# Later scale matmuls and later weight splits in the first MLP product, and an earlier g_mem_post product in the memory rows

## The chip, the cores and the metric

The kernel runs on one core of one Trainium2 chip. The metric is the device time of one execution in microseconds (us), measured over several runs of the same program; a further execution is profiled. The engines are TensorE (PE in the profile), VectorE (DVE), ScalarE (ACT), GpSimd (POOL) and SyncE (SP), whose queue here issues the loads and stores.

## The reference

One layer of a streaming encoder, on x of 1024 rows by 1024 columns. In outline:

```
x = x + rmsnorm(concat(rmsnorm(fox), rmsnorm(chunked)) @ w_out, g_mix_post)   # two attention groups
h = rmsnorm(x, g_mem_pre)
y = memory_cross_attention(h, rmsnorm(mem, g_mem_kv), w_mq, w_mk, w_mv, w_mo) # 4 heads, 256 memory rows
x = x + rmsnorm(y, g_mem_post)
h = rmsnorm(x, g_ff_pre)
y = square(relu(h @ w_ff1)) @ w_ff2                                           # 1024 -> 4096 -> 1024
x = x + rmsnorm(y, g_ff_post)
```

`rmsnorm(x, g)` is x / sqrt(mean(x^2) + 1e-6) * g. All inputs and the result are float32. The change touches the end of the memory attention (its norm, the residual, the next norm) and the first product of the MLP, here FF1.

## The kernel before, in words

A float32 product is made of three float16 ones: each operand is split into a high part (ACT's activation, `split_hi`, L2520) and a low part, value minus high part (DVE, `split_lo`, L2523), and `mm3` (L230 to L232) sums high x high, low x high and high x low in one PSUM bank. Before it is split a weight is multiplied by a scale that comes from its squares. FF1 and FF2 are moreover done by a two by two scheme with seven products in place of eight, so sums of operands and results (s1 to s4, u2, u3, g11, g22) stand on DVE and POOL.

Up to the memory attention a planner sets the order of the work. The part here, from the last rows of the memory attention on, is written under `tc.manual_schedule()`: each engine does its instructions in the order in which the program text issues them, and an instruction that waits holds up all that stands behind it on its engine. The same is true of SP's queue.

**The rows.** The second half of the rows comes in four blocks b of 128. For each, `ym` is a product of 24 matmuls; `row_out` (L2696 to L2700) squares it on ACT (L1248), multiplies its right half by g_mem_post on DVE (L2699) and takes the inverse root of the mean square on POOL (h3y, L1253 to L1256). `row_sum` (L2702 to L2707) adds it to the residual `xth` on DVE (L2703), stores the sum and squares it on ACT, and POOL takes the next inverse root (h3x). `row_norm` (L2710) multiplies by it and by g_ff_pre. `residual_in` loads `xth`. Then the rows are transposed (`Turn`, PE's trx), and summed and split for the seven products.

**FF1.** The 4096 columns are worked as 16 pairs j of two blocks of 128, a pair in seven products of 12 matmuls. `first_row` makes the first two, px and py; for pairs 0 to 6 (`AHEAD` = 7) they are made early, between the rows, and put by; from pair 7 on at the head of the pair. Then come the products T2 (into px, and from pair 7 on added to what px holds), T1 (into pz), T3 (px), T4 (pv) and B22 (pz). ACT copies px out three times: p (L2583), u after T2 (L2986) and u after T3 (L3004; before pair 7 DVE's L3002 stands for it). DVE then makes g22 from pz and that u (L3006). `Weights` holds the weights of a pair: `squares` (ACT, jn, L2771), `scales` (PE's nw of two small matmuls, L2777; DVE's rowsc, L2778; POOL's roots and factors, L2779 to L2782), and `split(n)` for n = "a" (whi_a, wlo_a), "s23" (v..hi, v..lo), "s1a" and "s4" (u..hi, u..lo). While pair j is worked, pair j+1's weights are scaled and split, and pair j+2's are squared; two rows of FF2's weights are squared in each pair too (w2n, L1311). At pair 14 the norms of all features and of FF2's weights are taken (L1384 to L1401).

Of the kernel before, what the change touches and what calls it, by code (L numbers as in the profile page):

```python
# [165 lines left out]
def layer(tc, out, t):  # L166
    nc = tc.nc
    ctx = ExitStack()
    with ctx:
        build(ctx, tc, nc, out, t)  # L170


def build(ctx, tc, nc, out, t):
# [13 lines left out]
    def mm_tile(shape, name, tag="mm"):  # L187
        return psp.tile(shape, F32, tag=tag, bufs=2, name=name)
# [39 lines left out]
    def mm3(ps, lh, ll, rh, rl, start, stop, more=False):  # L228

        nc.tensor.matmul(ps, lh, rh, start=start, stop=False, skip_group_check=more)  # L230
        nc.tensor.matmul(ps, lh, rl, start=False, stop=False, skip_group_check=more)  # L231
        nc.tensor.matmul(ps, ll, rh, start=False, stop=stop, skip_group_check=more)  # L232
# [1013 lines left out]
    def square_sum(x, ss, n=1024, scale=1.0 / 32.0):  # L1246
        junk = p2.tile([P, D], BF16, tag="junk", bufs=1, name="junk")
        nc.scalar.activation(junk[:, :n], x, AF.Square, scale=scale, accum_out=ss)  # L1248

    def inverse_rms(a, name, b=None):  # L1250
        r = small.tile([P, 1], F32, tag="rstd", bufs=8, name=name)
        if b is None:
            nc.gpsimd.tensor_scalar(r, a, EPS, None, op0=ALU.add)  # L1253
        else:
            nc.gpsimd.tensor_scalar(r, a, b, EPS, op0=ALU.add, op1=ALU.add)
        nc.gpsimd.tensor_tensor(r, r, mhalf[:, 0:1], op=ALU.pow)  # L1256
        return r
# [979 lines left out]
    with tc.manual_schedule():  # L2237
# [87 lines left out]
        ps = mm_tile([P, 4], "ssx", "pv")  # L2325
# [149 lines left out]
    AHEAD = 7  # L2475
# [6 lines left out]
    def t2(name):  # L2482
        if region[0]:
            return pr.tile([P, HT], F32, tag="t2", bufs=9, name=name)
        return pf.tile([P, HT], F32, tag="t2", bufs=18, name=name)
# [3 lines left out]
    def bank(name, tag=None):  # L2489
        if tag is None:  # L2490
            tag = ("mm", "s", "tr", "pv")[banks[0] % 4]
            banks[0] += 1
        return mm_tile([P, HT], name, tag)
# [12 lines left out]
    def raw_w(src, name):  # L2506
        raw = wp.tile([P, D], F32, tag="wraw", bufs=3, name=name)
        nc.sync.dma_start(raw, src)
        return raw
# [20 lines left out]
    def product(ps, w, off, blk, more=False):  # L2530
        for kc in range(4):
            c = slice(off + kc * P, off + (kc + 1) * P)
            xh, xl = blk.at(kc)
            mm3(ps, w.hi[:, c], w.lo[:, c], xh, xl, kc == 0 and not more, kc == 3, more)

    def ff1_raw(fb):
        return raw_w(t["w_ff1"][fb].rearrange("p a b -> p (a b)"), f"wf{fb}")
# [154 lines left out]
    def residual_in(b):  # L2692
        xts[b] = p2.tile([P, D], F32, tag="xt", bufs=2, name=f"xth3{4 + b}")
        nc.sync.dma_start(xts[b], x1d[4 + b])

    def row_out(b, ps):  # L2696

        square_sum(ps, ss[b][:, 1:2], HT, um32)
        nc.vector.tensor_tensor(y[b][:, HT:], ps, gmpost[:, HT:], op=ALU.mult)  # L2699
        rx[b] = inverse_rms(ss[b][:, 0:1], f"h3y{4 + b}", ss[b][:, 1:2])  # L2700

    def row_sum(b):  # L2702
        nc.vector.scalar_tensor_tensor(xts[b], y[b], rx[b], xts[b], op0=ALU.mult, op1=ALU.add)  # L2703
        nc.sync.dma_start(x2d[4 + b], xts[b])
        s2 = small.tile([P, 1], F32, tag="ss", bufs=8, name=f"s2h3{4 + b}")
        square_sum(xts[b], s2)
        rx[b] = inverse_rms(s2, f"h3x{4 + b}")  # L2707

    def row_norm(b):
        nc.vector.scalar_tensor_tensor(y[b], xts[b], rx[b], gffpre, op0=ALU.mult, op1=ALU.mult)  # L2710

    manual = ExitStack()
    manual.enter_context(tc.manual_schedule())
    residual_in(0)
    raws = {}
    for b in range(4):
        c = slice(b * P, (b + 1) * P)
        ps = mm_tile([P, HT], f"ym11{b}", "tr" if b < 2 else "pv")
        for kp in range(4):
            for j in range(2):  # L2720
                mm3(ps, o[kp][0][:, j, c], o[kp][1][:, j, c], wo[kp][0][:, j, :], wo[kp][1][:, j, :],
                    kp == 0 and j == 0, kp == 3 and j == 1)
        if b:
            row_sum(b - 1)
            row_norm(b - 1)
        if b < 3:
            raws[EARLY + b] = ff1_raw(EARLY + b)
            residual_in(b + 1)
            row_out(b, ps)
    units = [Turn(a, i) for a in range(2) for i in range(2)]  # L2730
    add = {}
    units[0].turn()
    row_out(3, ps)
    units[0].sums()
    add[0] = ahead(0)
    row_sum(3)
# [82 lines left out]
    cur, nxt = Weights(0), Weights(1)  # L2819
# [128 lines left out]
    with manual:  # L2948
        sums, stores, norms, puts = (lambda: []), [], [], []
        for j in range(NP):  # L2950
            more = j + 1 < NP
            after = Weights(j + 2) if j + 2 < NP else None
            w = cur.w
            late = more and 0 < j < AHEAD
# [20 lines left out]
                fetch(3)  # L2975
                prepare(0)
            product(x, w["s23"], 0, XT["T2"], more=j >= AHEAD)
            if more and j + 1 >= AHEAD:
                nxt.scales()
            put_off = j < PUT_OFF  # L2980
            both = u4(f"ug{j}", (P, 2, HT), F32) if put_off else None
            u2 = both[:, 0, :] if put_off else t2(f"u2_{j}")
# [6 lines left out]
            put(j, 0, g11)  # L2989
            z = bank(f"pz{j}")  # L2990
            product(z, w["s1a"], 0, XT["T1"])
            if late:
                nxt.sums(nc.vector)
            if more:
                if j + 1 >= AHEAD:
                    nxt.split("a")
                if j and not late:
                    nxt.split("s23")
            product(x, w["s23"], HT, XT["T3"], more=True)
            u3 = p1 if put_off else t2(f"u3_{j}")  # L3000
            if j < AHEAD:
# [2 lines left out]
                nc.scalar.activation(u3, x, AF.Copy)  # L3004
            g22 = both[:, 1, :] if put_off else t2(f"g22_{j}")
            nc.vector.tensor_add(g22, z, u3)  # L3006
            stores = [form() for form in forms[:1]]
            if late:
                nxt.sum4(nc.vector)
# [60 lines left out]
            cur, nxt = nxt, after  # L3070
# [266 lines left out]
```

## Time and profile before

| | us |
|---|---|
| median of 3 runs (lowest to highest) | 1436.27 (1435.35 to 1437.5) |
| the profiled execution | 1439.24 |
| its span | 1437.4 |
| PE busy in it | 1398.9 (97%) |
| DVE, ACT, POOL busy | 1163.8 (81%), 1010.9 (70%), 527.4 (37%) |
| mean granted clock of PE | 0.992 |

A share of busy time is a mean over stages. What an edit is worth is read where it stands: which engine waits there, for what, and what comes after. In a row of the trace the first figure is the start in us from the span's start, the second the duration, then come engine, line, operation, written tile, read tiles and shape; in brackets the idle time of that engine before it and what ended that time. The row blocks lie at 780 to 860 us, the early first products up to some 880, the pairs 0 to 6 up to 979, the pairs 7 to 15 up to some 1150; FF2 follows to the end.

### The profile page before, as it was taken

To read this page: it belongs to the slowest core of one execution; us is meant where nothing else is said; L and a number is where in the kernel's file an instruction comes from. 1 tells how busy PE (TensorE), PEld (TensorE's weight loads), DVE (VectorE), ACT (ScalarE), POOL (GpSimd) and SP (SyncE) were. 2 spreads that over 40 slices of the span, in tenths; PEclk is the share of its full clock that TensorE was granted. 3 is DMA by queue.
4 is the path that set the end of the run, shared out by engine and by line. 5 is a ranking of instruction groups with operands and counts; after the bars stand their busy time and mean duration, and the time that the engine had idled before them with its cause. 6 is when DMAs were issued, how large, how long until landed. Compare 5 with 4: busy or idle time off the path is not lost. (4 is left out here: it accounts for less than half of the span.)

```text
span 1437.4 us, 22722 instructions
## 1 busy us (share of the span) xinstructions
PE 1398.9 (97%) x7723; PEld 866.2 (60%) x7723; DVE 1163.8 (81%) x1886; ACT 1010.9 (70%) x1750; POOL 527.4 (37%) x679
## 2 busy tenths in 40 slices
PE   8989999999999999999999999999999999999997
PEld 8746666666668887855556544444444445666653
DVE  7887877777778755889888877777988987899998
ACT  6767888978778775686466555786887657665654
POOL 2467777787655433451113421003344100000003
PEclk9999999999999999999999999999999999999999
DMA  7142454345424566461325446976888998686885
GB/s 281 49 128 75 131 165 165 112 122 164 137 74 139 174 233 235 174 235 49 103 81 169 143 170 241 339 240 203 271 289 281 323 382 306 238 306 224 312 300 205
DMA packets 116214, 286.31 MB, mean 199 GB/s; under 512 B 13161, under 2 KB 31601, under 8 KB 116097
## 3 DMA queue, kind: packets, MB, share of 16 engines
q1 hardware_dynamic: 115952, 284.59, 58.7%
q8 instruction: 61, 1.00, 0.3%
q14 instruction: 57, 0.46, 0.1%
q10 hardware_dynamic: 144, 0.26, 0.1%
HBM read 210.82 MB, written 65.59 MB: 192 GB/s over the span
## 5 line engine op out<-in xcount | busy, mean ns | idle before, releaser
L3104 POOL TENSOR_SCALAR rf<-sf 128x1 f32<-128x1 f32 x7 | 6.4, 912 | 280.7 <-ACT jf L3083 280.4
L870 ACT ACTIVATE phl<-ptr 128x512 f16<-128x512 f32 (+3 forms) x152 | 80.9, 537 | 38.4 <-PE ptr L860 35.7
L1910 POOL TENSOR_SCALAR mp<-mp,mst 128x256 f32<-128x256 f32 x32 | 22.6, 716 | 121.1 <-DVE mst L1909 110.1
L866 DVE SCALAR_TENSOR_TENSOR phl<-ptr,phl 128x384 f16<-128x384 f32 (+1 forms) x76 | 46.8, 617 | 14.9 <-ACT phl L870 14.2
L868 DVE TENSOR_TENSOR phl<-ptr,phl 128x384 fp32r<-128x384 f32 (+1 forms) x76 | 46.5, 617 | 9.5 <-ACT phl L870 8.8
L230 PE MATMUL yw<-whiwo,yT_hi 128*128 128x512 f32 x128 | 51.3, 401 | 2.7 <-DVE yw L1625 2.7
L2943 ACT ACTIVATE vhif<-ra,fsc 128x1024 f16<-128x1024 f32 x34 | 38.9, 1143 | 19.4 <-PE fx L232 9.2
L2943 ACT ACTIVATE whif<-ra,fsc 128x1024 f16<-128x1024 f32 x34 | 38.9, 1144 | 19.3 <-PE fx L232 12.0
L2945 DVE SCALAR_TENSOR_TENSOR vhif<-ra,fsc,vhif 128x1024 f16<-128x1024 f32 x34 | 43.6, 1282 | 10.0 <-ACT vhif L2943 9.7
L907 PE MATMUL pv<-phl,vs 128*128 128x512 f32 (+1 forms) x152 | 50.9, 421 | 0.0
L231 PE MATMUL yw<-wlowo,yT_hi 128*128 128x512 f32 x128 | 50.6, 395 | 0.0
L232 PE MATMUL yw<-whiwo,yT_lo 128*128 128x512 f32 x128 | 50.4, 394 | 0.0
L230 PE MATMUL q<-hF_hi,wq 128*128 128x512 f16 x128 | 49.0, 383 | 0.7 <-DVE qs L1011 0.7
L230 PE MATMUL fx<-vlof,vhif 128*128 128x512 f16 x128 | 48.5, 379 | 0.8 <-DVE yc L3155 0.8
L230 PE MATMUL k<-hF_hi,wk 128*128 128x512 f16 x128 | 49.3, 385 | 0.0
L231 PE MATMUL q<-hF_lo,wq 128*128 128x512 f16 x128 | 48.5, 379 | 0.6 <-DVE hF_lo L2231 0.6
L231 PE MATMUL k<-hF_lo,wk 128*128 128x512 f16 x128 | 49.0, 383 | 0.0
L2945 DVE SCALAR_TENSOR_TENSOR whif<-ra,fsc,whif 128x1024 f16<-128x1024 f32 x34 | 43.6, 1281 | 6.4 <-ACT whif L2943 6.3
L232 PE MATMUL k<-hF_hi,wk 128*128 128x512 f16 x128 | 48.8, 381 | 0.0
L232 PE MATMUL q<-hF_hi,wq 128*128 128x512 f16 x128 | 48.5, 379 | 0.2 <-POOL wq L571 0.2
L230 PE MATMUL fx<-wlof,whif 128*128 128x512 f16 x128 | 48.5, 379 | 0.0
L231 PE MATMUL fx<-wlof,whif 128*128 128x512 f16 x128 | 48.5, 379 | 0.0
(906 smaller groups left out, 5372.3 us busy)
## 6 DMA issues: line engine op xcount, KB each, us to landing
wg<-in_w_ff SPq DMA_DIRECT2D x48, 512.0 KB, 5.7
ra<-gd SPq DMA_DIRECT2D x40, 512.0 KB, 5.3
wf<-in_w_ff SPq DMA_DIRECT2D x38, 512.0 KB, 4.4
w2n<-in_w_ff SPq DMA_DIRECT2D x32, 512.0 KB, 5.5
wi<-in_w_ff2q SPq DMA_DIRECT2D x28, 512.0 KB, 6.0
gd<-s SPq DMA_DIRECT2D x32, 256.0 KB, 5.0
wn<-in_w_ff SPq DMA_DIRECT2D x14, 512.0 KB, 4.5
gd<-g SPq DMA_DIRECT2D x19, 256.0 KB, 4.5
```

The lines of the kernel that those rows point to most:

```text
L230: nc.tensor.matmul(ps, lh, rh, start=start, stop=False, skip_group_check=more)
L231: nc.tensor.matmul(ps, lh, rl, start=False, stop=False, skip_group_check=more)
L232: nc.tensor.matmul(ps, ll, rh, start=False, stop=stop, skip_group_check=more)
L866: flow.put("V", at, 0.68, lambda: nc.vector.scalar_tensor_tensor(pl[:, live, :], tr[:, live, :], 2.0 ** 14, ph[:, live, :], op0=ALU.mult, ...
L868: if ph.dtype == F16 else nc.vector.tensor_sub(pl[:, live, :], tr[:, live, :], f(ph[:, live, :])), done, 1)
L870: flow.put("S", flow.end, 0.6, lambda ph=ph, tr=tr, live=live: nc.scalar.activation(ph[:, live, :], tr[:, live, :], AF.Copy, scale=2.0 ** ...
L907: nc.tensor.matmul(pv[:, :, qs_, :], v, hl[:, :, hs, :], start=c == 0 and turn == 0, stop=last)
L1910: mul = lambda st=st, pr=pr: nc.gpsimd.tensor_scalar(pr, pr, st[:, 2:3], 1.0, op0=ALU.mult, op1=ALU.mult)
L2943: nc.scalar.activation(ah, ra, AF.Copy, scale=su)
L2945: nc.vector.scalar_tensor_tensor(al, ra, su, ah, op0=ALU.mult, op1=ALU.subtract)
L3104: nc.gpsimd.tensor_scalar(r, ssf[b][:, 0:1], ssf[b][:, 1:2], EPS, op0=ALU.add, op1=ALU.add)
```

## The change

Two things are moved; nothing is added and nothing is taken away.

In the row blocks, the product with g_mem_post of block b+1 (`row_out`) stands ahead of the norm of block b (`row_norm`), the sum of a block follows at once, and the residual of block 1 is loaded together with that of block 0. In FF1, for pairs 6 to 14, `nxt.scales()` stands behind the T1 product and no longer behind the T2 product, and the splits "a" and "s23" of the next pair stand behind the T3 product's reading (u and g22) and no longer before it.

```diff
--- before.py
+++ after.py
@@ -2712,6 +2712,7 @@
     manual = ExitStack()
     manual.enter_context(tc.manual_schedule())
     residual_in(0)
+    residual_in(1)
     raws = {}
     for b in range(4):
         c = slice(b * P, (b + 1) * P)
@@ -2720,17 +2721,18 @@
             for j in range(2):
                 mm3(ps, o[kp][0][:, j, c], o[kp][1][:, j, c], wo[kp][0][:, j, :], wo[kp][1][:, j, :],
                     kp == 0 and j == 0, kp == 3 and j == 1)
-        if b:
-            row_sum(b - 1)
-            row_norm(b - 1)
         if b < 3:
+            row_out(b, ps)
+            if b:
+                row_norm(b - 1)
+                residual_in(b + 1)
             raws[EARLY + b] = ff1_raw(EARLY + b)
-            residual_in(b + 1)
-            row_out(b, ps)
+            row_sum(b)
     units = [Turn(a, i) for a in range(2) for i in range(2)]
     add = {}
+    row_out(3, ps)
+    row_norm(2)
     units[0].turn()
-    row_out(3, ps)
     units[0].sums()
     add[0] = ahead(0)
     row_sum(3)
@@ -2975,8 +2977,6 @@
                 fetch(3)
                 prepare(0)
             product(x, w["s23"], 0, XT["T2"], more=j >= AHEAD)
-            if more and j + 1 >= AHEAD:
-                nxt.scales()
             put_off = j < PUT_OFF
             both = u4(f"ug{j}", (P, 2, HT), F32) if put_off else None
             u2 = both[:, 0, :] if put_off else t2(f"u2_{j}")
@@ -2989,13 +2989,10 @@
             put(j, 0, g11)
             z = bank(f"pz{j}")
             product(z, w["s1a"], 0, XT["T1"])
+            if more and j + 1 >= AHEAD:
+                nxt.scales()
             if late:
                 nxt.sums(nc.vector)
-            if more:
-                if j + 1 >= AHEAD:
-                    nxt.split("a")
-                if j and not late:
-                    nxt.split("s23")
             product(x, w["s23"], HT, XT["T3"], more=True)
             u3 = p1 if put_off else t2(f"u3_{j}")
             if j < AHEAD:
@@ -3004,6 +3001,11 @@
                 nc.scalar.activation(u3, x, AF.Copy)
             g22 = both[:, 1, :] if put_off else t2(f"g22_{j}")
             nc.vector.tensor_add(g22, z, u3)
+            if more:
+                if j + 1 >= AHEAD:
+                    nxt.split("a")
+                if j and not late:
+                    nxt.split("s23")
             stores = [form() for form in forms[:1]]
             if late:
                 nxt.sum4(nc.vector)
```

DVE at the last three row blocks, before (xth is the residual and sum, ym the product, L2699 the g_mem_post product, L2703 the sum, L2710 the norm):

```order
L2703 SCALAR_TENSOR_TENSOR xth_9891<-ym_9370,h3y_9925,xth_9891 128x1024
L2710 SCALAR_TENSOR_TENSOR ym_9370<-xth_9891,h3x_9958,g_ff_pre 128x1024
L2699 TENSOR_TENSOR ym_9371<-ym_9928,g_mem_post 128x512
L2703 SCALAR_TENSOR_TENSOR xth_9920<-ym_9371,h3y_9969,xth_9920 128x1024
L2710 SCALAR_TENSOR_TENSOR ym_9371<-xth_9920,h3x_10002,g_ff_pre 128x1024
L2699 TENSOR_TENSOR ym_9372<-ym_9972,g_mem_post 128x512
L2703 SCALAR_TENSOR_TENSOR xth_9964<-ym_9372,h3y_10013,xth_9964 128x1024
L2710 SCALAR_TENSOR_TENSOR ym_9372<-xth_9964,h3x_10046,g_ff_pre 128x1024
L2699 TENSOR_TENSOR ym_9373<-ym_10016,g_mem_post 128x512
```

and now:

```order
L2703 SCALAR_TENSOR_TENSOR xth_9891<-ym_9370,h3y_9923,xth_9891 128x1024
L2699 TENSOR_TENSOR ym_9371<-ym_9936,g_mem_post 128x512
L2710 SCALAR_TENSOR_TENSOR ym_9370<-xth_9891,h3x_9933,g_ff_pre 128x1024
L2703 SCALAR_TENSOR_TENSOR xth_9893<-ym_9371,h3y_9964,xth_9893 128x1024
L2699 TENSOR_TENSOR ym_9372<-ym_9980,g_mem_post 128x512
L2710 SCALAR_TENSOR_TENSOR ym_9371<-xth_9893,h3x_9977,g_ff_pre 128x1024
L2703 SCALAR_TENSOR_TENSOR xth_9968<-ym_9372,h3y_10008,xth_9968 128x1024
L2699 TENSOR_TENSOR ym_9373<-ym_10024,g_mem_post 128x512
L2710 SCALAR_TENSOR_TENSOR ym_9372<-xth_9968,h3x_10021,g_ff_pre 128x1024
```

The product L2699 of a block moved from behind the norm L2710 of the block before to ahead of it.

PE in pair 6, at the end of the T2 product (px) and the beginning of the T1 product (pz), before:

```order
L231 MATMUL px_11158<-T_lo,v0hi_s_11098 128x512
L232 LDWEIGHTS v0lo_s_11099
L232 MATMUL px_11158<-T_hi,v0lo_s_11099 128x512
L2777 MATMUL nw_11171<-wsq,o_83 128x1 x2
L230 LDWEIGHTS whi_s1a_11121
L230 MATMUL pz_11189<-T_hi,whi_s1a_11121 128x512
```

and now, at the end of the T1 product and the beginning of the T3 product (px):

```order
L231 MATMUL pz_11181<-T_lo,whi_s1a_11121 128x512
L232 LDWEIGHTS wlo_s1a_11122
L232 MATMUL pz_11181<-T_hi,wlo_s1a_11122 128x512
L2779 MATMUL nw_11194<-wsq,o_83 128x1 x2
L230 LDWEIGHTS v0hi_s_11098
L230 MATMUL px_11158<-T_hi,v0hi_s_11098 128x512
```

The small matmuls nw moved behind 12 matmuls.

ACT in pair 8, from the end of g11 on, before (L3004 is the copy u after T3, whi_a and v1hi are split high parts of pair 9's weights, w2n squares):

```order
L2541 ACTIVATE g_8_11499<-g_8_11499 128x512
L2520 ACTIVATE whi_a_11552<-wf_11284,rowsc 128x1024
L2520 ACTIVATE v1hi_s_11556<-sc_11453,rowsc 128x1024
L3004 ACTIVATE u_8_11572<-px_11471 128x512
L1311 ACTIVATE w2n_11286,wsq<-w2n_11286 128x1024
L1311 ACTIVATE w2n_11288,wsq<-w2n_11288 128x1024
L2520 ACTIVATE whi_s1a_11601<-wf_11395,rowsc 128x1024
L2540 ACTIVATE g_8_11574<-g_8_11574,rowsc 128x512
L2541 ACTIVATE g_8_11574<-g_8_11574 128x512
```

and the same place now, where the copy is L3001:

```order
L2541 ACTIVATE g_8_11499<-g_8_11499 128x512
L3001 ACTIVATE u_8_11564<-px_11471 128x512
L2520 ACTIVATE whi_a_11568<-wf_11284,rowsc 128x1024
L2520 ACTIVATE v1hi_s_11572<-sc_11453,rowsc 128x1024
L1311 ACTIVATE w2n_11286,wsq<-w2n_11286 128x1024
L1311 ACTIVATE w2n_11288,wsq<-w2n_11288 128x1024
L2520 ACTIVATE whi_s1a_11601<-wf_11395,rowsc 128x1024
L2540 ACTIVATE g_8_11566<-g_8_11566,rowsc 128x512
L2541 ACTIVATE g_8_11566<-g_8_11566 128x512
```

The copy u moved ahead of the two split parts, which stand behind it now. The order behind these rows, up to the squares jn and the copy p of pair 9's px, is the same in both.

DVE from g11 of pair 7 (L2585) to the low parts of pair 8, before (rowsc is made from nw, g by L3006 is g22):

```order
L2585 TENSOR_TENSOR g_7_11318<-py_11303,p_7_11316 128x512
L2778 TENSOR_SCALAR rowsc<-nw_11332 128x1
L3050 TENSOR_TENSOR s_6_11344<-u_6_11179,g_6_11224 128x512
L3056 TENSOR_TENSOR u_6_11179<-p1r_11104,u_6_11179 128x512
L3058 TENSOR_TENSOR s_6_11347<-s_6_11344,p1r_11104 128x512
L3060 TENSOR_TENSOR s_6_11348<-u_6_11222,s_6_11347 128x512
L2523 SCALAR_TENSOR_TENSOR wlo_a_11372<-wf_11152,rowsc,whi_a_11371 128x1024
L2523 SCALAR_TENSOR_TENSOR v0lo_s_11376<-sc_11278,rowsc,v0hi_s_11375 128x1024
L3006 TENSOR_TENSOR g_7_11393<-pz_11358,u_7_11391 128x512
```

and now, with all lines behind the moved text two or three numbers off (rowsc L2780, the sums L3052 to L3062, g22 L3003):

```order
L2585 TENSOR_TENSOR g_7_11318<-py_11303,p_7_11316 128x512
L3052 TENSOR_TENSOR s_6_11336<-u_6_11171,g_6_11220 128x512
L3058 TENSOR_TENSOR u_6_11171<-p1r_11104,u_6_11171 128x512
L3060 TENSOR_TENSOR s_6_11339<-s_6_11336,p1r_11104 128x512
L3062 TENSOR_TENSOR s_6_11340<-u_6_11218,s_6_11339 128x512
L2780 TENSOR_SCALAR rowsc<-nw_11363 128x1
L3003 TENSOR_TENSOR g_7_11385<-pz_11350,u_7_11383 128x512
L2523 SCALAR_TENSOR_TENSOR wlo_a_11388<-wf_11152,rowsc,whi_a_11387 128x1024
L2523 SCALAR_TENSOR_TENSOR v0lo_s_11392<-sc_11278,rowsc,v0hi_s_11391 128x1024
```

rowsc moved behind the four sums, and g22 ahead of the two low parts.

## The prediction

> **What bounds the kernel now.** I read the page first, then TensorE's waits stage by stage, then the instructions around each of those waits. The page says that TensorE (PE) is the engine that sets the time:
>
> ```profile
> span 1437.4 us, 22722 instructions
> PE 1398.9 (97%) x7723; PEld 866.2 (60%) x7723; DVE 1163.8 (81%) x1886; ACT 1010.9 (70%) x1750; POOL 527.4 (37%) x679
> ```
>
> PE is idle for 38.5 us of 1437.4, so only what removes or adds PE idle time (or halves its clock) counts. PE's waits in the two stretches that the change touches, first 780 to 880 us (rows of the memory attention and the first rows of FF1), then 960 to 1130 us (pairs 6 to 14 of FF1), then all that follows:
>
> ```profile
> PE px L230 <- ACT whi_a L2520: 2.3, 1, 2.3
> PE px L232 <- DVE wlo_a L2523: 0.7, 1, 0.7
> ...
> PE nw L2777 <- ACT jn L2771: 1.8, 2, 1.0
> PE pz L230 <- DVE g L3006: 1.3, 2, 1.0
> ...
> PE py L230 <- DVE fsc L1384: 0.5, 1, 0.5
> ```
>
> The columns are total, times, longest. Waits that the edits can reach come to some 6 us; that is all there is to win beside the clock. Nothing in a stretch of 170 us with 1.3 us of `pz` waits leaves room for a large gain, but anything that comes late there is paid in full.
>
> **Term 1, the rows.** The product with g_mem_post (L2699) now stands ahead of the norm (L2710). One row of before on DVE, ACT and POOL:
>
> ```profile
> 826.39 1.28 DVE L2703 SCALAR_TENSOR_TENSOR xth<-ym,h3y,xth 128x1024 f32<-128x1024 f32 x1
> 829.92 1.29 DVE L2710 SCALAR_TENSOR_TENSOR ym<-xth,h3x,g_ff_pre 128x1024 f32<-128x1024 f32 x1 [2.25 <-POOL h3x L1256]
> 831.12 0.69 DVE L2699 TENSOR_TENSOR ym<-ym,g_mem_post 128x512 f32<-128x512 f32 x1
> 832.05 1.28 DVE L2703 SCALAR_TENSOR_TENSOR xth<-ym,h3y,xth 128x1024 f32<-128x1024 f32 x1 [0.25 <-POOL h3y L1256]
> ...
> 829.53 0.19 ACT L1248 ACTIVATION_READ_ACCUMULATOR junk<-ym,mfx 128x1 f32 x1
> ...
> 829.00 0.23 POOL L1253 TENSOR_SCALAR h3x<-s2h 128x1 f32<-128x1 f32 x1 [4.31 <-ACT junk L1248]
> 829.98 1.39 POOL L1255 TENSOR_SCALAR h3y<-ssm 128x1 f32<-128x1 f32 x1
> 831.46 0.56 POOL L1256 TENSOR_TENSOR h3y<-h3y,mhalf 128x1 f32<-128x1 f32 x1
> ```
>
> A row takes 832.05 - 826.39 = 5.66 us. POOL's small h3y operation takes 1.39 beside the norm where its like for h3x takes 0.23 alone, and the next sum waits for it. In the new order the product waits for ACT's square of the same bank (829.53 + 0.19 = 829.72), starts at about 829.75 and gives way to the norm 0.60 later, at 830.35 instead of 829.92. By then POOL's h3y operation has run unhindered (from 829.9, with some 0.1 between operations) and its root, 0.56, is just begun; the norm is issued over in 1.20 (831.12 - 829.92), so the next sum comes at 831.55 instead of 832.05. That is 0.5 us a row, for two rows, and 0.2 at the last one, about 1.2 us at the sums of the first turn. If the norm wins against the root, the root is done after it and nothing is gained.
>
> The Trainium skill, "SBUF — State Buffer", Who interferes with whom, says that a VectorE operation with two SBUF inputs and a GpSimd one exclude each other and that whoever issues first runs whole. The 1.39 against 0.23 agrees with it; it makes this term 1.2 or 0 by a margin of about 0.1 us.
>
> What it is worth to PE is less. PE is next late for the split weights of row 3 (the 2.3 and 0.7 above), and after that DVE has hardly a gap, as busy times by stretch show (PE, PEld, DVE, ACT, POOL, granted clock, DMA share, GB/s):
>
> ```profile
> 858.80:864.80 6.00, 6.00 (x15) 2.14 (x16) 5.91 (x9) 1.56 (x4) 0.00 (x0) 0.50 0.72 204
> ```
>
> I take -0.8 (between -1.2 and 0). The earlier residual load (xth1) only moves ahead of two weight loads on SP's queue; the first of PE's needs of those is not late in the waits above, so it is 0. The 0.50 clock costs some 3 us here; a wait shortened from 2.3 to 1.5 might avoid it (to -4), a chance I keep for the range.
>
> **Term 2, pair 6.** Before the z product PE stands for the squares of pair 7:
>
> ```profile
> 964.64 0.38 PE L232 MATMUL px<-T_hi,v0lo_s 128*128 128x512 f16 x1
> 965.98 0.38 PE L2777 MATMUL nw<-wsq,o 128*128 128x1 f32 x2 [0.95 <-ACT jn L2771]
> 967.16 0.58 PE L2777 MATMUL nw<-wsq,o 128*128 128x1 f32 x2 [0.80 <-ACT jn L2771]
> 971.65 0.38 PE L230 MATMUL px<-T_hi,v0hi_s 128*128 128x512 f16 x1
> ...
> 966.92 0.19 ACT L2771 ACTIVATION_READ_ACCUMULATOR jn<-wf 128x1 f32 x1
> ```
>
> At full clock the 12 matmuls of a product take 2.59 (term 3's rows have 36 of them and nw in 8.13). Moved behind the z product, nw comes at 964.86 + 2.59 = 967.45, when ACT's last square (966.92 + 0.19 = 967.11) is there: no wait, some 0.37 for nw itself (its row has 0.38), third product at 967.82 instead of 971.65. That is -3.8 us: 1.75 of waits, 1.46 of z product at the low clock that followed them (4.05 instead of 2.59), 0.6 of nw's broken run. Bounds: -3.8, and -2.2 if the clock falls anyway. The price is that the scales of pair 7 now come on DVE behind two sums of some 0.6, as L2699's row has them, while its first product is three products (7.8 us) away; this fits.
>
> **Term 3, the splits behind the bank's reading.** `split("a")` of the next pair now stands behind the copy u3 on ACT and behind g22 on DVE. On DVE that is good: the two `pz` waits, 1.3 us, were g22 standing behind wlo_a and vlo. They go: -1.3. On ACT it makes a ring. From pair 7 on, the T2 product adds into the bank of px, so it must wait until ACT has copied px out (p, L2583), and p is the last thing in ACT's order of a pair. ACT and PE of before, pair 7 to pair 9:
>
> ```profile
> 992.93 0.60 ACT L3004 ACTIVATE u<-px 128x512 f32<-128x512 f32 x1 [0.32 <-PE px L232]
> 993.43 1.05 ACT L1311 ACTIVATE w2n<-w2n 128x1024 f32<-128x1024 f32 x1
> ...
> 1010.68 1.15 ACT L2520 ACTIVATE whi_a<-wf,rowsc 128x1024 f16<-128x1024 f32 x1 [0.63 <-POOL rowsc L2781]
> 1012.78 0.57 ACT L3004 ACTIVATE u<-px 128x512 f32<-128x512 f32 x1
> ...
> 1021.94 0.58 ACT L2583 ACTIVATE p<-px 128x512 f32<-128x512 f32 x1
> ...
> 992.73 0.38 PE L230 MATMUL pv<-T_hi,whi_s1a 128*128 128x512 f16 x1
> ...
> 1003.09 0.38 PE L230 MATMUL px<-T_hi,v0hi_s 128*128 128x512 f16 x1
> 1011.22 0.38 PE L230 MATMUL pv<-T_hi,whi_s1a 128*128 128x512 f16 x1
> 1015.00 0.38 PE L230 MATMUL pz<-B_hi,u0hi_s 128*128 128x512 f16 x1 [1.03 <-DVE g L3006]
> 1022.77 0.38 PE L230 MATMUL px<-T_hi,v1hi_s 128*128 128x512 f16 x1
> ```
>
> PE's own pair is 1022.77 - 1003.09 - 1.03 = 18.65 us. ACT is only just in time: p ends at 1022.52, T2 starts at 1022.77. From whi_a on ACT then runs without a gap to p: 1010.68 to 1022.52, 11.84 us, of which the copy u is 0.50 (993.43 - 992.93, as long as it holds ACT), so 11.34 for the rest. In the new order whi_a cannot start before u3's copy, and that not before T3 is done. T3 is done 1011.22 - 1003.09 = 8.13 after T2's start (nw is in it before as after), the copy begins 992.93 - 992.73 = 0.20 later and holds ACT for 0.50. So whi_a starts 8.83 after T2's start, p ends 8.83 + 11.34 = 20.17 after it, and only then can the T2 of the next pair start. The ring is 20.17 against 18.65: 1.52 us lost in each pair for which the ACT work is the same. How many these are, groups of ACT between 985 and 1123 us tell:
>
> ```profile
> L2771 ACT ACTIVATE jn<-wf 128x1024 bf16<-128x1024 f32 x14 | 14.7, 1049 | 0.3
> L1311 ACT ACTIVATE w2n<-w2n 128x1024 f32<-128x1024 f32 x14 | 14.6, 1045 | 0.0
> ```
>
> Two of each in a pair: seven pairs, 7 x 1.52 = +10.6. From 14 to 15 the two jn (2.2) are missing, 18.0, no loss. What hid this work of ACT so far was that whi_a and vhi ran beside T3; that cover is gone. Bounds: 0 if whi_a need not wait so (I see nothing that would allow it: ACT runs in order), +13 if 0.3 more a pair comes between.
>
> On DVE, rowsc now stands behind the four sums s1 to s4 too:
>
> ```profile
> 1008.50 0.14 DVE L2778 TENSOR_SCALAR rowsc<-nw 128x1 f32<-128x1 f32 x1
> ...
> 1010.60 0.69 DVE L3060 TENSOR_TENSOR s<-u,s 128x512 f32<-128x512 f32 x1
> ```
>
> In this pair, where DVE is late from put-off sums, rowsc would come at 1010.60 + 0.69 = 1011.29, and whi_a 1010.68 - 1008.50 = 2.18 later at 1013.5, 1.6 after the copy lets it go (1011.9). The ring's own delay gives DVE back up to 1.5 of that. I take +0.8, between 0 and 1.6 for each of the two or three pairs with such a backlog (0 to +4).
>
> **Term 4, the end of FF1.** The norms of the features are read on DVE behind the last splits of pair 15, and PE's py waits for that reading:
>
> ```profile
> 1126.55 1.14 ACT L2520 ACTIVATE whi_s1a<-wf,rowsc 128x1024 f16<-128x1024 f32 x1
> ...
> 1132.33 0.19 DVE L1384 TENSOR_REDUCE fsc<-norms 128x1 f32<-128x32 f32 x1
> ...
> 1115.64 0.38 PE L230 MATMUL px<-T_hi,v0hi_s 128*128 128x512 f16 x1
> ```
>
> whi_s1a comes 10.91 after T2's start now; then 8.83 + 1.04 + 1.04 + 2.09 (whi_a, vhi, two w2n) = 13.0, so 2.1 later, with DVE's lo parts, its sums and L1384 behind it in a row. PE's wait of 0.5 becomes 2.6: +2.1, between 0 and 4.
>
> **The sum**: -0.8 - 3.8 - 1.3 + 10.6 + 0.8 + 2.1 = +7.6 us. The profiled execution took 1439.24 (span 1437.4), 3.0 above the median of the runs; on it the change gives 1446.8, on the median of 1436.27 it gives 1443.9.
>
> **Rivals.** (a) It works as one would wish: ACT keeps up, no ring. Then the gains stand alone, -0.8 - 3.8 - 1.3 = -5.9: 1430.4. For it speaks that ACT is only 70% busy; against it, that its order is fixed and p is already within 0.25 us of being late. (b) Gains and losses cancel: the ring is only 19.0 long (1.2 us less of ACT's work in it), 7 x 0.35 + 0.8 + 2.1 = 5.4 against -5.9: about 1436. (c) Worse: each wait of 1.5 to 3 us in the ring also halves the clock. In the rows 1.75 us of waits did so for a stretch that cost 1.46, and 3 us of waits for one of 3 us; on four of seven pairs that adds 6: 7.6 + 6: about 1450. The Trainium skill, "TensorE: Matmul & The Clock Gate", Part 1, has a free-running window of about 3.4 us and asks for an idle window of that length before the clock falls; by it no wait of the ring would do so and (c) would be void. Here 0.63 was granted (967.60 to 971.65) behind two waits that sum to 1.75, so the trace doesn't bear that out:
>
> ```profile
> 967.60:971.65 4.05, 4.05 (x13) 1.53 (x14) 3.80 (x7) 3.56 (x6) 2.32 (x4) 0.63 1.00 328
> ```
>
> **Chances.** The forecast (ring, +5 to +12) 0.55, (c) 0.15, (b) 0.11, (a) 0.19. A difference under 0.2% (2.9 us) is no change: faster 0.19, same 0.11, slower 0.70. The likeliest case alone is 1441 to 1449. The range reaches 1431.5 to 1453, into (a) below and over (c), with about 0.13 left out below and 0.07 above.
>
> **What would show it.** In the changed profile: no nw wait at pair 6 and clock 1 there (term 2); no `pz <- DVE g` waits; in their place a wait of PE's px for ACT's p (L2583) of some 1.5 us, seven times, in pairs that take 20.2 us instead of 18.65, with ACT's whi_a right behind its u copy; a py wait of about 2.6 for the norms' reading; the rows 0.5 us closer. The forecast is wrong if p ends before py's last matmul does, pair after pair, or if whi_a starts well before u3's copy.

## The result and the profile after

The changed kernel takes 1453.6 us (median of 4 runs, 1452.49 to 1454.42) against 1436.88 (4 runs, 1435.35 to 1438.03): ratio 1.0117, 95% interval 1.0099 to 1.0134. It is 16.7 us slower. The prediction had the sign and the ring, but 1443.9, +7.6 us, with a range that ended at 1453.0.

The two profiled executions took 1439.24 (span 1437.4) and 1453.6 (span 1451.8), so the traces differ by 14.4; the other 2.3 us is that the profiled execution of before stood that much above its median. TensorE's waits in the changed kernel, from 780 to 880, 960 to 1130 and 1130 to 1170 us:

```profile
PE px L232 <- DVE wlo_a L2523: 1.8, 3, 0.9
...
PE px L230 <- ACT whi_a L2520: 1.4, 2, 0.9
...
PE px L230 <- ACT p L2583: 14.3, 8, 2.8
...
PE norms L1393 <- ACT u L2541: 4.2, 1, 4.2
```

The waits for nw (1.8) and for g (1.3) are gone. In the rows the wait of 2.3 for row 3's whi_a is gone too, but five waits of at most 0.9 for split weights stand there now, 3.2 us in all where it was 3.0 in two. New are eight waits of PE for ACT's copy p, 14.3 us in all, and one of 4.2 us ahead of the second norms. The products at which p is waited for, pair 7 to pair 14 (the two left out have 1.81 as well):

```profile
978.80 0.38 PE L230 MATMUL px<-T_hi,v1hi_s 128*128 128x512 f16 x1 [0.62 <-ACT p L2583]
999.27 0.38 PE L230 MATMUL px<-T_hi,v0hi_s 128*128 128x512 f16 x1 [1.81 <-ACT p L2583]
1020.76 0.38 PE L230 MATMUL px<-T_hi,v1hi_s 128*128 128x512 f16 x1 [2.84 <-ACT p L2583]
1042.90 0.38 PE L230 MATMUL px<-T_hi,v0hi_s 128*128 128x512 f16 x1 [1.80 <-ACT p L2583]
1063.36 0.38 PE L230 MATMUL px<-T_hi,v1hi_s 128*128 128x512 f16 x1 [1.81 <-ACT p L2583]
...
1124.74 0.38 PE L230 MATMUL px<-T_hi,v0hi_s 128*128 128x512 f16 x1 [1.81 <-ACT p L2583]
```

From start to start this is the account. A pair takes 1063.36 - 1042.90 = 20.46 us and stays so to the end, where PE's own work is 18.49 (before, undisturbed: 1078.66 - 1060.17). Where the time went, by the same product in both traces (before less after, or the other way):

| | us |
|---|---|
| all ahead of what was changed (a ym matmul at 784.55, then at 783.75) | -0.80 |
| from there to the T2 product of pair 6 (177.72 to 175.78) | -1.94 |
| pair 6 (third product at 971.65, then 965.08) | -3.83 |
| new wait for p at pair 7 (0.62; 0.78 from start to start) | +0.78 |
| waits for g gone (19.68 and 18.91 in place of 18.49) | -1.61 |
| seven pairs of 20.46 in place of 18.49 | +13.79 |
| one of them 1.03 longer (pair 8 to 9, DVE late) | +1.03 |
| halved clock in pair 9, behind the wait of 2.84 | +1.68 |
| end of FF1, from the norms to the T3 product of pair 15 | +5.5 |
| sum, against 14.4 of the spans | +14.6 |

The first line belongs to the two executions and not to the change. The second is the rows' share in these two executions only (see the rows alone, below). In pair 8 DVE is late: three of its operations in a row take 1.64 to 1.76 us, in the middle of POOL's sums, where such an operation takes 0.69 elsewhere. One of them, and what POOL does meanwhile:

```profile
1001.15 1.64 DVE L2596 TENSOR_TENSOR s<-ug 128x512 f32<-128x512 f32 x1
...
1000.65 1.60 POOL L2798 TENSOR_TENSOR sc<-wf,wf 128x512 f32<-128x512 f32 x1
```

ACT, DVE and POOL in one pair of the changed kernel show what holds whi_a, and so p:

```profile
1066.64 0.71 ACT L2540 ACTIVATE u<-u,rowsc 128x512 f32<-128x512 f32 x1
1067.38 0.63 ACT L2541 ACTIVATE u<-u 128x512 f32<-128x512 f32 x1
...
1071.69 0.60 ACT L3001 ACTIVATE u<-px 128x512 f32<-128x512 f32 x1 [2.39 <-PE px L232]
1072.42 1.15 ACT L2520 ACTIVATE whi_a<-wf,rowsc 128x1024 f16<-128x1024 f32 x1
...
1083.19 0.58 ACT L2583 ACTIVATE p<-px 128x512 f32<-128x512 f32 x1
...
1068.05 0.69 DVE L3052 TENSOR_TENSOR s<-u,g 128x512 f32<-128x512 f32 x1 [2.11 <-ACT u L2541]
...
1070.71 0.15 DVE L2780 TENSOR_SCALAR rowsc<-nw 128x1 f32<-128x1 f32 x1
...
1072.20 0.19 POOL L2783 TENSOR_SCALAR rowsc<-rowsc 128x1 f32<-128x1 f32 x1
```

The copy u starts 8.33 us after T2's start (1063.36), as predicted. whi_a starts 0.73 after it, not 0.50: it waits for POOL's scale (done at 1072.39), which waits for rowsc, which stands on DVE behind s1 to s4, and s1 waits for ACT's square of u2 (done at 1068.01). From whi_a to the end of p it is 11.35 us. Two paths run through this ring, ACT's own order and the scale's way over DVE and POOL, and they end within 0.23 us of each other. The last 0.05 of the 20.46 lie between the end of p and the start of T2.

The norms at the end of FF1 on PE, before the change, when the second (L1393) followed the first at once:

```profile
1128.95 0.30 PE L1383 MATMUL norms<-wsq,o 128*128 128x32 f32 x2
1129.09 0.39 PE L1393 MATMUL norms<-wsq,o 128*128 128x32 f32 x2
```

The same in the changed kernel, on PE and then DVE:

```profile
1138.05 0.30 PE L1383 MATMUL norms<-wsq,o 128*128 128x32 f32 x2
1142.53 0.61 PE L1393 MATMUL norms<-wsq,o 128*128 128x32 f32 x2 [4.18 <-ACT u L2541]
...
1141.70 0.68 DVE L3040 TENSOR_TENSOR u<-pz,u 128x512 f32<-128x512 f32 x1
```

and the stretches behind its two longest waits (columns as in the prediction: stretch, length, busy times of the five engines, granted clock, DMA share, GB/s):

```profile
1020.70:1025.10 4.40, 4.34 (x13) 1.67 (x13) 4.37 (x5) 0.01 (x1) 3.59 (x3) 0.61 0.60 207
1142.90:1147.80 4.90, 4.90 (x15) 1.88 (x15) 3.26 (x18) 0.00 (x0) 1.10 (x2) 0.55 0.44 148
```

The row names ACT's u, which ended last, at 1142.44, but the norms use nothing of it. DVE's reading of pair 14's pz ended at 1141.70 + 0.68 = 1142.38, and by the program text the second norms were put into the bank of that pz. Both norms always take one of the two banks with the tag `pv`. nw, pz and most other products take their tags in turn (`bank`), so with nw behind pz the two swap places: before the change nw of pair 14 had that bank, and it had long been read; now pz of pair 14 has it. (An experiment below tests this.)

### The profile page after: what moved, and what is told of

Read it like the earlier page. It is cut to its first block, busy times and chain, and to the rows that moved or that the text cites. A ratio compares the mean times of both kernels' runs of the same rounds, so it can differ in the third digit from the quotient of the medians.

```text
span 1451.8 us, 22718 instructions
## 1 busy us (share of the span) xinstructions
PE 1400.4 (96%) x7723; PEld 867.0 (60%) x7723; DVE 1163.1 (80%) x1886; ACT 1011.6 (70%) x1750; POOL 515.5 (36%) x679
```

## The experiments

Each was run beside the kernel before on the same chip; ratios are to it. The changed kernel itself was not run again, so times are compared with its 1453.6 across occasions, on which the median of the kernel before differed by up to 1.4 us.

**Rows alone.** The four row blocks as in the change, FF1 as before.

> The rows alone (FF1 as before). Theory, from the two traces: the T2 product of pair 6 starts 2.7 us earlier (959.5 against 962.3 us) because a row takes about 5.2 instead of 5.66 us, PE's wait for row 3's split weights falls from 2.3 to about 0.9 us and the clock is not halved there, of which some 1.3 us is given back in later waits; so 2.7 us under the kernel before, about 1434. Rival, the prediction as recorded: the row part is worth 0.8 us and the rest came from elsewhere, about 1436.

Measured: 1435.27 against 1437.13, ratio 0.9992 (0.9981 to 1.0004): not told apart from no change. In its trace T2 of pair 6 starts at 958.04, 4.2 ahead of before. That is no measure of the rows: 1.6 of it were there at the ym matmul ahead of all that was changed (782.96 against 784.55), and with the old row order T2 of pair 6 starts anywhere from 958.69 (scales alone) to 962.27 (before). From that ym matmul to T2 of pair 6 it takes 176.6 to 177.7 us in the four profiles with the old row order, and 175.1 to 178.9 in the ten with the new one; the middle values are 177.0 and 175.9. So the rows are worth some 1 us, with a spread as large. PE's waits for split weights are not fewer (2.8 us in five pieces against 3.0 in two), but shorter, 0.9 at most instead of 2.3. The clock goes with that. Between 855 and 865 us it was halved in all four profiles with the old row order (before, scales alone, splits alone, pair 6 alone) and in none of the ten with the new one.

**Scales alone.** Only this, splits and rows as before:

```diff
             product(x, w["s23"], 0, XT["T2"], more=j >= AHEAD)
-            if more and j + 1 >= AHEAD:
-                nxt.scales()
...
             product(z, w["s1a"], 0, XT["T1"])
+            if more and j + 1 >= AHEAD:
+                nxt.scales()
```

> Scales behind the T1 product, splits and rows as before. Theory (a ring PE - scales - ACT - PE): nw now ends 5.5 us after T2's start, whi_a can start some 2.1 to 2.3 later at 7.7, and from whi_a ACT takes 11.84 to the end of p, so p ends 19.5 after T2's start against PE's 18.5: a wait for p of about 1 us in each of seven pairs (+7), pair 6 gains 3.8, and the bank rotation gives a wait for the second norms at pair 14 of 3 us or more: 1441 to 1446. Rival (only the place of the splits closes the ring, this move is the good half): pair 6's 3.8 us alone, about 1433, with no wait for p.

Measured: 1464.12, ratio 1.0191 (1.0170 to 1.0212). Both theories fall: it is the worst of all, 27 us slower, and not by a wait for p. PE's waits from 960 to 1135 us are one line:

```profile
PE pz L230 <- DVE g L3006: 19.5, 8, 2.5
```

and DVE in one pair shows why:

```profile
1032.38 0.15 DVE L2778 TENSOR_SCALAR rowsc<-nw 128x1 f32<-128x1 f32 x1
1035.28 1.28 DVE L2523 SCALAR_TENSOR_TENSOR wlo_a<-wf,rowsc,whi_a 128x1024 f16<-128x1024 f32 x1 [2.75 <-ACT whi_a L2520]
1036.48 1.28 DVE L2523 SCALAR_TENSOR_TENSOR v0lo_s<-sc,rowsc,v0hi_s 128x1024 f16<-128x1024 f32 x1
1037.68 0.68 DVE L3006 TENSOR_TENSOR g<-pz,u 128x512 f32<-128x512 f32 x1
```

With rowsc late and the splits still ahead of g22, DVE itself stands idle for whi_a (2.75) with g22 queued behind the low parts, and the B22 product, whose bank pz must be read first, waits 2.0 to 2.5 us in each of the nine pairs 6 to 14, with halved clock behind four of them. So the later scales need the later splits; the two moves were made for each other, and neither is the good half.

**Splits alone.**

```diff
-            if more:
-                if j + 1 >= AHEAD:
-                    nxt.split("a")
-                if j and not late:
-                    nxt.split("s23")
             product(x, w["s23"], HT, XT["T3"], more=True)
...
             nc.vector.tensor_add(g22, z, u3)
+            if more:
+                if j + 1 >= AHEAD:
+                    nxt.split("a")
+                if j and not late:
+                    nxt.split("s23")
```

> Splits behind T3's reading, scales and rows as before. Theory: whi_a right behind the copy u, without a wait for POOL, so the ring is 8.13 + 0.20 + 0.50 + 11.34 + 0.05 = 20.2 us instead of 18.5: seven waits for p of about 1.7 us (+12), the pz waits of 1.6 gone, pair 6 unchanged, py's wait at the end longer by about 2: about 1448 to 1450. No wait of the second norms on PE at pair 14, since the banks rotate as before. Rival (the late scales are what holds whi_a back, the splits' place costs little): under 1439.

Measured: 1451.28, ratio 1.0098 (1.0081 to 1.0114). The ring is as expected to a tenth; the time is 1.3 us above the 1448 to 1450. PE's waits from 960 to 1135 us (beside those for nw), and then two T2 products and ACT ahead of the second:

```profile
PE px L230 <- ACT p L2583: 10.9, 7, 1.6
```

```profile
1062.82 0.38 PE L230 MATMUL px<-T_hi,v1hi_s 128*128 128x512 f16 x1 [1.55 <-ACT p L2583]
1083.02 0.38 PE L230 MATMUL px<-T_hi,v0hi_s 128*128 128x512 f16 x1 [1.55 <-ACT p L2583]
...
1071.14 0.60 ACT L2999 ACTIVATE u<-px 128x512 f32<-128x512 f32 x1 [2.40 <-PE px L232]
1071.64 1.14 ACT L2520 ACTIVATE whi_a<-wf,rowsc 128x1024 f16<-128x1024 f32 x1
```

whi_a follows the copy by 0.50, the ring is 1083.02 - 1062.82 = 20.20, seven waits. PE waits 2.6 us at py for the first norms at the end, behind which the clock is halved once (the product takes 4.27 instead of 2.59), and not at all for the second. This is the ring of the prediction by itself; the scales' move adds 0.26 a pair to it.

**p ahead of the squares jn.** The changed kernel, with pair j+2's two squares issued behind pair j+1's copy p (and POOL's sums of the next pair, which overwrite what they read, behind them):

```diff
                 x, _, g11, add = first_row(j, w["a"])
+                if squared:
+                    squared.squares()
+                    nxt.sums()
+                    nxt.sum4()
                 add()
...
-            if after and after.j >= AHEAD:
+            if after and after.j == AHEAD:
                 after.squares()
+            squared = after if after and after.j > AHEAD else None
```

> The changed kernel with the two squares jn of pair j+2 put behind the copy p of pair j+1 on ACT (pairs 8 on; POOL's sums of the next pair behind them). Theory: the ring loses jn's 2.2 us, 20.46 - 2.2 = 18.2, under PE's 18.5: the waits of px for ACT's p vanish (14.3 us, and 1.7 of halved clock), the end with the wait for the second norms (4.2, and 2.2 of clock) stays: about 1438. Rival (the loss is not ACT's queue ahead of p but the late weights themselves, wlo_a and v): the waits go to other products, and the time stays above 1448.

Measured: 1447.04, ratio 1.0066 (1.0051 to 1.0081). Less than half of what I expected: waits for p fall from 14.3 to 6.9, and the wait for the second norms, which was to stay, grows from 4.2 to 5.9. ACT's whi_a now waits for POOL, here in one pair:

```profile
1064.81 0.60 ACT L3005 ACTIVATE u<-px 128x512 f32<-128x512 f32 x1 [2.05 <-PE px L232]
1067.01 1.15 ACT L2520 ACTIVATE whi_a<-wf,rowsc 128x1024 f16<-128x1024 f32 x1 [1.60 <-POOL rowsc L2783]
```

POOL's sums, now later, run beside DVE's s1 and u2, which take 1.16 and 1.64 us instead of 0.69; rowsc and the scale come that much later. With ACT's queue 2.2 us shorter, the other path holds whi_a.

**The old bank rotation.** The changed kernel with nw's bank taken ahead of pz's, the matmul left where the change has it:

```diff
             product(x, w["s23"], 0, XT["T2"], more=j >= AHEAD)
+            nwb = bank(f"nw{j + 1}") if more and j + 1 >= AHEAD else None
...
-                nxt.scales()
+                nxt.scales(nwb)
```

> The changed kernel with the PSUM bank for nw taken where it was before the change (so the banks rotate as before), the matmul itself where the change has it. Theory: PE's 4.2 us for the second norms at pair 14 are a bank that pair 14's pz still holds until DVE has made u2; with the old rotation they go, PE waits at py for the first norms' reading instead (2.6, as with the splits alone), and of the 9.6 us from the norms to py some 4 are won: about 1449.5. Rival (the norms wait for work, not for a bank): the same time as the changed kernel, 1453.6, with the wait only renamed.

Measured: 1449.87, ratio 1.0085 (1.0071 to 1.0099), 3.7 under the changed kernel. The theory had 1449.5; that the total met it is in part luck. The ring is untouched (waits for p are 14.0 us in eight). In the trace the end of FF1, from the norms to T3 of pair 15, takes 15.0 us, where it took 17.4 in the changed kernel and 11.9 before: the bank is worth 2.4 us. Another 1.7 is the clock in pair 9, which stayed at 1 this time behind the same wait of 2.84. PE there and at the end of FF1:

```profile
1020.88 0.38 PE L230 MATMUL px<-T_hi,v1hi_s 128*128 128x512 f16 x1 [2.84 <-ACT p L2583]
...
1136.66 0.39 PE L1393 MATMUL norms<-wsq,o 128*128 128x32 f32 x2
...
1142.48 0.59 PE L230 MATMUL py<-h3T_hi,whi_a 128*128 128x512 f16 x1 [2.84 <-DVE fsc L1384]
```

The second norms (L1393) wait no more, so their wait was for a bank; behind it stands the wait at py that the prediction had (2.6).

**The squares w2n behind p.** The changed kernel with the two squares of FF2's weights taken out of ACT's stretch from u3 to p, for pairs 7 to 13 (`held` is issued behind p of the next pair):

```diff
-            for norm in due[:2]:
-                norm()
+            if AHEAD <= j < NP - 2:
+                held = due[:2]
+            else:
+                for norm in due[:2]:
+                    norm()
```

> The changed kernel with the two squares w2n of FF2's weights (2.1 us) moved on ACT from between the split parts to behind the copy p, for pairs 7 to 13; no other engine waits for them there. Theory (ACT's queue between u3's copy and p is the ring): 20.46 - 2.1 = 18.4, under PE's 18.5, so the seven waits for p shrink to some tenths, the halved clock in pair 9 goes too, the end stays as it is: about 1438 to 1440. Rival (the path nw - rowsc - POOL - whi_a holds the ring, ACT's queue behind it is filler): waits for p stay above 1 us each, time above 1446.

Measured: 1446.15, ratio 1.0055 (1.0041 to 1.0069). Between the two: five waits are left, 7.0 us, at the T2 products of pairs 7, 8, 9, 11 and 13. Ahead of the last three ACT waits for DVE; here for pair 11:

```profile
1054.41 0.71 ACT L2520 ACTIVATE u1hi_s<-sd,rowsc 128x512 f16<-128x512 f32 x1
1056.96 0.72 ACT L2540 ACTIVATE u<-u,rowsc 128x512 f32<-128x512 f32 x1 [1.84 <-DVE u L3038]
```

u3 less pv (L3038) stands on DVE behind g22, the two low parts, in every second pair four sums of an earlier pair (1.5 us), and wlo_s1a. The pairs without those sums (to 10, 12 and 14) ran without a wait, so ACT's queue was what had held them. The wait at pair 8 (1.86) has another cause: ACT's second jn stood 1.84 us for the load of its weight.

**Those sums behind u3 less pv.** The same kernel with one more move:

```diff
-            stores = [form() for form in forms[:1]]
...
             nc.vector.tensor_sub(u3, u3, v)
+            for form in forms[:1]:
+                form()()
```

> The kernel of the w2n experiment with DVE's four put-off sums (1.5 us, in every second pair) moved from ahead of wlo_s1a to behind u3 less pv. Theory: the waits for p that stayed in every second pair (1.5 each) are ACT's relu of u3 waiting for DVE, which stands behind those sums; they go, all pairs run at PE's 18.5, and only the wait for the second norms stays: 7 less, about 1439. Rival (the waits have another cause, DMA or POOL's sums): 1446 as without the move.

Measured: 1446.78, ratio 1.0064 (1.0050 to 1.0078). No gain; the wait for the second norms is 6.1 us here, against 4.3 without the move. The wait at ACT's relu of u3 fell from 1.84 to 0.38, as the theory said, but the waits for p moved to the other pairs (7.0 us, five again). There DVE's tail is longer by the moved sums, rowsc is late, and whi_a waits for POOL (ACT in one of them):

```profile
1064.56 0.60 ACT L3004 ACTIVATE u<-px 128x512 f32<-128x512 f32 x1
1067.34 1.15 ACT L2520 ACTIVATE whi_a<-wf,rowsc 128x1024 f16<-128x1024 f32 x1 [2.18 <-POOL rowsc L2783]
```

With the old bank rotation besides:

> The same with the old bank rotation. Theory: the wait for the second norms goes as it did alone (-3.7), so about 1435, which is the change with its ring and its bank mended: under the kernel before by about 3 us, the gain of rows and pair 6 less 2 us at the end of FF1. Rival: 1438 or more, since the end of FF1 waits for DVE's reading of the first norms instead.

Measured: 1443.78, ratio 1.0043 (1.0029 to 1.0057). The norms' wait goes again, but py then waits 4.2 us for the first norms, and the ring's 7.2 us stay. The ring was not mended by moving single pieces.

**Pair 6 alone.** The kernel before with the change's FF1 order in pair 6 only:

```diff
-            if more and j + 1 >= AHEAD:
+            if more and j + 1 > AHEAD:
                 nxt.scales()
...
             product(z, w["s1a"], 0, XT["T1"])
+            if more and j + 1 == AHEAD:
+                nxt.scales()
...
-                if j + 1 >= AHEAD:
+                if j + 1 > AHEAD:
                     nxt.split("a")
...
             nc.vector.tensor_add(g22, z, u3)
+            if more and j + 1 == AHEAD:
+                nxt.split("a")
```

> The kernel before with the change's FF1 order in pair 6 alone (scales behind T1, split behind g22), all other pairs and the rows as before. Theory: pair 6 loses its two waits for nw and the low clock behind them, 3.8 us in the trace, and no ring exists before pair 7: about 1433.3. Rival (what pair 6 wins is given back in pairs 7 to 9, whose weights then come late): within 1 us of the kernel before, 1436 to 1437.

Measured: 1435.47 against 1438.25, ratio 0.9981 (0.9970 to 0.9991): 2.8 us faster, a new wait of 0.6 for p at pair 7 off the 3.8.

**Pair 6 and the rows.**

> The new row order and the change's FF1 order in pair 6 alone; pairs 7 to 15 as before. Theory: the two gains measured apart add, about -1.9 (rows) and -2.8 (pair 6): 4 to 5 us under the kernel before, ratio about 0.997, no waits for p beyond the 0.6 of pair 7. Rival: an earlier PE only runs into DVE and ACT, which are not earlier, and the sum is no more than pair 6 alone (0.998).

Measured: 1434.23 against 1437.34, ratio 0.9977 (0.9968 to 0.9986): 3.1 us faster. The new order in pair 6, with or without the new rows, is the only part of the change that beats the kernel before by more than the intervals, and this is the best of the runs; what the rows add to pair 6 is within the intervals.

**Low parts behind g22, high parts where they were**, with rows and pair 6 as in the change. For pairs 7 to 14 `split("a")` and `split("s23")` make only the high part ahead of T3, and DVE's low parts follow g22. This was to win the 1.6 us of `pz` waits without ACT's ring.

> The new row order, the change's order in pair 6 alone, and in pairs 7 to 14 only the low parts (DVE) behind g22, while the high parts (ACT) and the scales stay where they were. Theory: rows -2 (as measured alone), pair 6 -3.8, the two pz waits -1.6, no wait for p, since ACT's order is that of before: about 1430. Rival: the low parts behind g22 wait for the copy u and come late for the next px, a new wait of PE's px for wlo_a, and the time is 1434 or more.

Measured: 1438.09, ratio 0.9999 (0.9988 to 1.0009). What rows and pair 6 give is lost again: g22 waits on DVE for the copy u (2.09 idle) with the low parts queued behind it, u3 less pv comes late, ACT's relu of u3 waits 1.40 for it, and p is late in three pairs besides pair 7 (4.1 us in all). py waits 1.8 at the end instead of 0.5. With the put-off sums behind u3 less pv as well:

> The kernel with rows, pair 6 and low parts behind g22 (high parts and scales as before) and the four put-off sums behind u3 less pv. Theory: the 4.1 us of waits for p in that kernel were ACT's relu of u3 behind the same sums; they go, and the time falls by about 4 to 1433 or 1434, ratio about 0.996. Rival: waits move to py or to the norms at the end of FF1, and the time stays at 1438.

Measured: 1441.78, ratio 1.0030 (1.0018 to 1.0042). Worse. The waits for p fall to 2.5, but waits of pz for g return (3.0) and py waits 2.9 at the end: the rival's way, and 4 us beyond its time.

## Why the prediction was right and where it was wrong

**Right.** The sign, and what causes it: T2 of the next pair waits for p, p stands at the end of ACT's order, and whi_a behind u3's copy makes that a ring longer than PE's pair. Splits alone show it by itself at 20.20 us, where the prediction worked out 20.17. Pair 6 (-3.8) came out to a tenth (-3.83), with some luck: 1.5 us of it were halved clock behind the waits for nw, and with the rows alone the same two waits (0.95 and 0.80) were not followed by it, so that only some 2.2 us stood there to be won. The waits for g vanished. The copies, counts and order that the text named are those in the trace. Rival (a), that ACT keeps up, is refuted by the seven profiles with high parts behind the copy in pairs 7 to 13, which have 6.9 to 14.3 us of waits for p; rival (b), a ring of 19.0, by the measured 20.20 and 20.46.

**Two steps failed: the size of the ring (term 3) and the end of FF1 (term 4).** For the ring the prediction had 7 x 1.52 = +10.6, at most +13, and it measured 13.8. Two parts of it were off:

- PE's own pair was taken as 19.68 - 1.03 = 18.65 us, from the one pair that held a wait. The row's idle figure is smaller than what the wait costs from start to start (1.19). Undisturbed pairs, which the trace has (1060.17 to 1078.66), give 18.49. That is 0.16 x 7 = 1.1 us.
- The ring was taken as 20.17 and is 20.46: 2.0 us over seven pairs. 0.23 of each is the scale's way over DVE and POOL, and 0.05 the step from p's end to T2's start. The prediction priced that path only for pairs with a backlog on DVE (+0.8); it left out that in every pair s1 waits for ACT's square of u2, so that rowsc, now behind s1 to s4, has a fixed place after T2 also without a backlog.

The extra pair with a late DVE cost 1.03 where 0.8 was put, and the clock was halved once behind it (1.68), which is rival (c) in one pair instead of four. (The stretch of 1.46 us that rival (c) puts into the rows is pair 6's.)

**The end of FF1** was +2.1 in the prediction, at most +4, and is +5.5. The wait that it named, py for the first norms, exists (2.6 with splits alone, 2.84 with the old banks). What stood in front of it in the changed kernel was not seen: the second norms in a bank that DVE had not read, 4.2 us, and the halved clock behind that. The prediction treated the move of nw as a move in PE's order alone; it also moves nw's turn in the banks. With the banks restored 2.4 us of the 5.5 came back; of the other 3.1 the longer wait at py is 2.3 and the halved clock behind it 1.3, less 0.5 for a short wait ahead of T3 that went.

**Term 1** was -0.8, and about -1 is what fourteen profiles show at the T2 product of pair 6, with a spread of the same size; the -1.94 between the two main profiles is more than that. The row's 5.66 became 5.16 us (predicted 5.16), with POOL's small operation at 0.30 instead of 1.39, as argued. DVE and POOL in a row of the changed kernel:

```profile
829.27 0.69 DVE L2699 TENSOR_TENSOR ym<-ym,g_mem_post 128x512 f32<-128x512 f32 x1 [2.08 <-ACT junk L1248]
829.88 1.27 DVE L2710 SCALAR_TENSOR_TENSOR ym<-xth,h3x,g_ff_pre 128x1024 f32<-128x1024 f32 x1
831.07 1.28 DVE L2703 SCALAR_TENSOR_TENSOR xth<-ym,h3y,xth 128x1024 f32<-128x1024 f32 x1
...
829.49 0.30 POOL L1255 TENSOR_SCALAR h3y<-ssm 128x1 f32<-128x1 f32 x1
```

PE's wait for row 3's whi_a is 0.91 instead of 2.27, with the clock at 1 behind it, which the prediction kept for the range and not for the sum. By the times alone the rows' gain is not resolved (0.9981 to 1.0004).

In the account of the traces the losses were put too small by 3.2 (ring), 0.2 (late DVE), 1.7 (clock) and 3.4 us (end of FF1), and a wait of 0.8 at pair 7 was put at nothing. Against that stand 1.1 us more in the rows, 0.3 more at the waits for g, and 0.8 that came ahead of the rows. The range's upper end rested on the forecast's own terms plus a halved clock, with no room for a wait that was not listed, and the median fell 0.6 above it.

What stays open is whether late splits could pay at all. In the changed order the paths through ACT, DVE and POOL end within some tenths of each other, so that easing one showed the next; no run shortened all of them together (jn and w2n, say, were never both behind p).

## What to carry to other kernels

When an operation is moved behind a reading on an engine that works in order, add up that engine's work from there to the last thing another engine waits for, and compare it with the period of the slowest engine, taken from an undisturbed round; a few tenths of slack in the trace of before say that there is no room for more. Then look for the second path of about the same length, since it holds the time as soon as the first is eased, and for what else moves with the operation: a buffer handed out in turn moves too. Two moves that each look like half of a gain can be costly alone (27 and 14 us here) and together (17), while the one place where the wait stood was worth 3 us.

## What the runs showed of the hardware that was not expected

The idle time that a row shows before a matmul is less than the time that is lost: 1.03 shown and 1.19 lost from start to start, 1.81 shown and 1.97 lost. The 0.16 is how the profile draws a matmul: its row is 0.38 long, and the next one in a product starts 0.22 after it.

The length of a wait does not by itself say whether the clock is halved behind it. It was behind single waits of 2.84 and 4.18 us in the changed kernel, behind 2.58 at py with splits alone, behind four of the nine waits of 2.0 to 2.5 us with scales alone, and behind 1.75 to 2.27 us in the rows, where another wait of 0.7 followed within 1.4 us. But with the old banks the same product as in the changed kernel waited the same 2.84 us, and the clock stayed at 1:

```profile
1020.80:1025.20 4.40, 4.32 (x21) 1.95 (x21) 4.40 (x4) 1.53 (x4) 3.62 (x3) 1.00 0.69 245
```

The waits of 0.95 and 0.80 us for nw were followed by a product of 4.05 us in the kernel before, of 4.27 with splits alone, and of 2.59 with rows alone. Behind the single waits of 1.55 and 1.81 us, a dozen of them, the clock was not halved. What decides it these runs do not show.

In the middle of POOL's sums of the same shape, DVE operations of 128x512 took 1.64 to 1.76 us where they otherwise take 0.69 (pair 8 of the changed kernel).

In the rows the clock stayed halved for more than one length: 6 us and more in the profile of before, some 3.4 us (from the mean of the stretch, 0.66 over 5 us) with scales alone and with splits alone. So a single execution can differ from another by some us through the clock alone.
